# mLSTM stage: state transfers on another queue, one head after the other, and a new order of matmuls inside a weight block

## The chip, the cores and the metric

One core of one Trainium2 chip runs the whole program in one launch. The metric is the device time of an execution in microseconds, the median over runs. Five engines work side by side, each through its own instructions in order: TensorE (PE in the profile, its weight loads PEld), VectorE (DVE), ScalarE (ACT), GpSimd (POOL) and SyncE (SP). An engine whose next instruction waits holds up everything behind it. DMA transfers are issued from the queue of one of the engines; before the change, all of them from SP's.

## The reference

One inference step of a two-layer decoder trunk, for a prompt of 256 tokens and 8 samples of one token each, which share the weights. Model width 2048, everything in float32. Cut to what matters:

```python
for i in range(2):
    mix = conformer_conv(x, ...) if i == 0 else mlstm_mixer(x, ...)
    x = layer_norm(ALPHA * x + mix, ...)
    x = layer_norm(ALPHA * x + conv_ffn(x, ...), ...)
    x = x + sigmoid(x @ pl_w_gate[i]) * rms_norm(p[i] @ pl_w_proj[i], pl_g[i])

# mlstm_mixer: 8 heads, q and k of width 128, v of width 256
z = x @ w_in                       # q, k, v, output gate o, input and forget gates
...
# for each chunk of 128 tokens and each head:
s   = (q @ k.T) * exp(d - m_tok)
num = s @ v + (q @ c) * w_inter
den = max(abs(sum(s) + (q @ n) * w_inter), exp(-m_tok))
h   = num / den
c   = g_state * c + (g_tok * k).T @ v     # matrix memory, 128 x 256 a head
n   = g_state * n + sum(g_tok * k)
...
hn  = (h - mean(h)) * rsqrt(var(h) + eps) * hn_g
out = (sigmoid(o) * hn) @ w_out + b_out
```

Each of the 8 samples brings its own matrix memory `c` for each head (8 x 8 x 128 x 256 floats, 8 MB), which is read, multiplied with q, updated and written back.

## The kernel before

Activations lie feature by feature: 128 features on the partitions, 264 columns (256 prompt tokens and 8 samples). A float32 product is made of three faster ones: the input is split in a high and a low part (XH, XL), each weight chunk too (`whi` on ACT, L238; `wlo` on DVE, L239), and TensorE adds high by high (L254), high by low input (L256 and L263) and low weight by high (L257) into one accumulator.

`wblock` (L203) does one block: 512 output features, four accumulators `acc` of 128 features, the input features in chunks of 128 (`kc`), two chunks to a half (four where the block is 256 wide). Weights come by `raw` tiles over SP's queue. `side` is a table from a chunk's number to functions that are called ahead of that half: in this way norms of the heads are put between the matmuls of a block. Six PSUM banks serve the accumulators, so a block's third and fourth accumulator take the banks that the first and second of the block before it leave. `lag` and `stage` are variants for the first blocks behind a layer norm and the last ahead of one.

The order on each engine is not the program's: a planner with a simulated timeline places the instructions by priority and by when it expects their inputs. `tc.high_priority` moves weight splits and evictions ahead. `after(a, b)` fixes that `a` stands behind `b` in order, without a wait.

The mLSTM stage (`mlstm`, L668) works on four pairs of heads. `project(pr)` makes q and k (one block), then v (one block), with evictions to `qk` (L905, L907) and `vv` (L925) on ACT. `heads(pr)` runs two `Head` objects through `turns`, which takes one step of each generator in turn: `prompt` (exponentials L770, scores, transposes, numerators, denominators, the prompt's final state) and `sample` (the products with the samples' states). `opened(pr)` makes the output gate (L943), `Head.norm` the norm over a head in three steps (`hm` L874, `hq` L882, then square root, reciprocal and product), and `gated` multiplies and splits into XH, XL as the input of `ml_w_out`. `out_blocks` (L444) does four blocks of 512 features and adds each into X (the residual).

During the heads the memory of X is lent out: X itself is put in DRAM (`xscr`, L695) and comes back ahead of `out_blocks` (L980). The lent room holds the samples' states `Ct` and the rows of q and k, `kb`, broadcast to all partitions: for each head two halves (`b4`) of four samples with a buffer each. The two heads of a pair, and all pairs, use the same two buffers in turn:

```python
for b4 in range(2):
    Ct, kb = ...                       # X's room
    dma.dma_start(Ct, I["cT"][h, :, 4 * b4:4 * b4 + 4])
    dma.dma_start(kb, rows[h, 4 * b4:4 * b4 + 4].partition_broadcast(P))
    ...                                # qp = Ct * q, sum -> qc       (DVE, L847, L849)
    ...                                # kb = k * v, eight copies     (ACT, L853)
    ...                                # Ct = Ct * f + kb, four       (DVE, L856)
    dma.dma_start(O["cT"][h, :, 4 * b4:4 * b4 + 4], Ct)
    yield
```

Of the kernel before, what the change touches and what calls it, by code (L numbers as in the profile page):

```python
# [14 lines left out]
AF = mybir.ActivationFunctionType  # L15
# [92 lines left out]
def _body(ctx, tc, nc, I, O):  # L108
# [85 lines left out]
                big.tile([P, 8, T], dt, name=name + "1", tag="hB1"))  # L194

    def split(hi, lo, src):
        s.copy(hi, src)
        tt(lo, src, f32(hi), ALU.subtract)

    wdma, wlast = [None], [None]  # L200

# [1 line left out]
    def wblock(W, cols, rhs, nk, acc, k0=0, loe=None, hook=None, fine=False, native=None, hold=(), lag=0, stage=0, side=None):  # L203
        behind, late = [], []
        width = sum(w for _, w in cols)
        nm = width // P
        kq = 4 if width == 256 else 2
        for kg in range(0, nk, 2 * kq):
            kn = min(2 * kq, nk - kg)
            raw = rawp.tile([P, 4, 512], F32, name="raw")  # L210
            if width == 256:
                raw = raw.rearrange("p a (b m) -> p (a b) m", b=2)
            for ka, step in ([(k, 2) for k in range(0, kn, 2)] if fine else [(0, kn)]):
                if hook:
                    hook(kg + ka, step)
                at = 0
                for c0, w in cols:
                    wdma[0] = dma.dma_start(raw[:, ka:ka + step, at:at + w],
                                  W[(k0 + kg + ka) * P:(k0 + kg + ka + step) * P, c0:c0 + w]
                                  .rearrange("(k p) m -> p k m", p=P))  # L220
                    at += w
            for h0 in range(0, kn, kq):
                for f in (side or {}).get(kg + h0, ()):
                    f()
                if native and native(kg + h0):
                    for kc in range(kg + h0, kg + h0 + kq):
                        for j in range(nm):
                            pe.matmul(acc[j], raw[:, kc - kg, j * P:(j + 1) * P], X[:, kc], start=kc == 0,  # L228
                                      stop=kc == nk - 1)
                    continue  # L230
                hi = hlp.tile([P, 2, 512], F32R, name="whi")
                lo = hlp.tile([P, 2, 512], F32R, name="wlo")
                if width == 256:
                    hi, lo = (w.rearrange("p a (b m) -> p (a b) m", b=2) for w in (hi, lo))
                r = raw[:, h0:h0 + kq, :width]
                e = loe(kg + h0) if loe else v
                with tc.high_priority(AHEAD):
                    whi = s.copy(hi[:, :, :width], r)  # L238
                    wlo = e.tensor_tensor(lo[:, :, :width], r, f32(hi[:, :, :width]), ALU.subtract)  # L239
                for k, first in hold:  # L240
                    if kg + h0 >= k:
                        after(whi, first[0])
                        after(wlo, first[1])
                if nk - kg - h0 <= stage:

                    late.append((kg + h0, hi, lo))
                    continue
                for k2 in range(kq):
                    kc = kg + h0 + k2
                    xh, xl = rhs(kc)  # L250
                    for j in range(nm):
                        wh = hi[:, k2, j * P:(j + 1) * P]
                        wl = lo[:, k2, j * P:(j + 1) * P]
                        pe.matmul(acc[j], wh, xh, start=kc == 0, stop=False)  # L254
                        if kc and not lag:
                            pe.matmul(acc[j], wh, xl, start=False, stop=False)  # L256
                        wlast[0] = pe.matmul(acc[j], wl, xh, start=False, stop=not lag and kc == nk - 1)  # L257
                    if kc == 0 or lag:
                        behind.append((kc, [hi[:, k2, j * P:(j + 1) * P] for j in range(nm)], xl))
                    while behind and (kc >= behind[0][0] + lag or kc == nk - 1):  # L260
                        k0_, whs, xl = behind.pop(0)
                        for j in range(nm):
                            pe.matmul(acc[j], whs[j], xl, start=False, stop=lag > 0 and k0_ == nk - 1)  # L263
        for j in range(nm if late else 0):
            for ka, hi, lo in late:
                for k2 in range(2):
                    xh, xl = rhs(ka + k2)
                    wh, wl = (w[:, k2, j * P:(j + 1) * P] for w in (hi, lo))
                    pe.matmul(acc[j], wh, xh, start=False, stop=False)
                    pe.matmul(acc[j], wh, xl, start=False, stop=False)  # L270
                    pe.matmul(acc[j], wl, xh, start=False, stop=ka + k2 == nk - 1)
# [396 lines left out]
    def mlstm(xin):  # L668
# [79 lines left out]
        NP = smp.tile([P, NH], F32, name="NP")  # L748
        NS = smp.tile([P, NH, NB], F32, name="NS")

        class Head:


            def __init__(self, h, j, qk, vv, H):
                self.h, self.q, self.k, self.v, self.H = h, qk[:, j], qk[:, 2 + j], vv[:, 2 * j:2 * j + 2], H
                self.bc = bc = s0[:, j * RP:(j + 1) * RP]
                dma.dma_start(bc, scr[h:h + 1, :].partition_broadcast(P))
                self.bw, self.ben, self.bwi, self.bwf = (bc[:, 256:384], bc[:, 384:648], bc[:, 648:656],
                                                         bc[:, 656:664])
                e = s0[:, 2 * RP + j * T:2 * RP + (j + 1) * T]  # L760
                self.E, self.den = e[:, :SEQ].rearrange("p (n l) -> p n l", n=2), e
                self.P = s1[:, j * 256:j * 256 + 256].rearrange("p (n l) -> p n l", n=2)
                self.vtag = ("sf", "fo")[j]

            def prompt(self):
                h, q, k, vh, E, Pt, H, den = self.h, self.q, self.k, self.v, self.E, self.P, self.H, self.den
                tt(E, self.bc[:, 0:SEQ].rearrange("p (n l) -> p n l", n=2),
                   mask.unsqueeze(1).to_broadcast([P, 2, L]), ALU.add)
                for n in range(2):
                    act(E[:, n], E[:, n], AF.Exp, bias=AT[:, n, h:h + 1], scale=-1.0)  # L770
                yield
                ps = misc("S")
                for n in range(2):
# [43 lines left out]
            def sample(self):  # L817
# [20 lines left out]
                yield  # L838
                qc = smp.tile([P, NB, 2], F32, name="qc", bufs=2)
                for b4 in range(2):  # L840
                    Ct, kb = (XF[:, o + b4 * 1024:o + b4 * 1024 + 1024].rearrange("p (b x k) -> p b x k", b=4, x=2)
                              for o in (0, 2048))
                    dma.dma_start(Ct, I["cT"][h, :, 4 * b4:4 * b4 + 4])
                    dma.dma_start(kb, rows[h, 4 * b4:4 * b4 + 4].partition_broadcast(P))
                    for b2 in (0, 2):
                        qp = s1[:, 512 + 4 * T:1024 + 4 * T].rearrange("p (b x k) -> p b x k", b=2, x=2)
                        ins = tt(qp, Ct[:, b2:b2 + 2], kb[:, b2:b2 + 2, 0:1, :].to_broadcast([P, 2, 2, P]), ALU.mult)  # L847
                        after(ins, self.pt)
                        v.tensor_reduce(qc[:, 4 * b4 + b2:4 * b4 + b2 + 2], qp, AX.X, ALU.add)  # L849
                    for bi in range(4):  # L850
                        e = 4 * b4 + bi
                        for x in range(2):
                            act(kb[:, bi, x], kb[:, bi, 1], AF.Copy, scale=vw[:, x, e:e + 1])  # L853
                    for bi in range(4):
                        e = 4 * b4 + bi
                        stt(Ct[:, bi], Ct[:, bi], bwf[:, e:e + 1], kb[:, bi], ALU.mult, ALU.add)  # L856
                    dma.dma_start(O["cT"][h, :, 4 * b4:4 * b4 + 4], Ct)
                    yield
                hs = H[:, :, SEQ:]
                tt(hs, qc.rearrange("p b x -> p x b"), bwf.unsqueeze(1).to_broadcast([P, 2, NB]), ALU.mult)  # L860
                sv = smp.tile([P, 2, NB], F32, name="sv", bufs=2)
# [37 lines left out]
        def project(pr, first=None, second=None):  # L899
# [22 lines left out]
            acc = proj([(2048 + pr * 512, 512)], second)  # L922
            with tc.high_priority(AHEAD):
                for j in range(4):
                    s.copy(vv[:, j], acc[j])  # L925
            return qk, vv

        def heads(pr, qk, vv):
# [3 lines left out]
                Hs = s1[:, 512:512 + 4 * T].rearrange("p (x t) -> p x t", x=4)  # L932
            hd = [Head(2 * pr + j, j, qk, vv, Hs[:, 2 * j:2 * j + 2]) for j in range(2)]
            turns([x.prompt() for x in hd] + [x.sample() for x in hd])
            return Hs, [x.norm() for x in hd]

        def opened(pr, side=None):

# [7 lines left out]
        def gated(pr, Hs, so, js):  # L946
            for j in js:
                c = 4 * pr + j
                stt(Hs[:, j], Hs[:, j], pc("ml_hn_g", c), so[:, j], ALU.mult, ALU.mult)
                split(XH[:, c], XL[:, c], Hs[:, j])  # L950

        def normed(*gens):

# [4 lines left out]
            return side  # L958

        p0 = project(0)  # L960
        h0, n0 = heads(0, *p0)
        so = opened(0)
        p1 = project(1, normed((n0[0], 6)), normed((n0[1], 6)))
        gated(0, h0, so, range(4))
        h1, n1 = heads(1, *p1)
        so = opened(1)
        p2 = project(2, normed((n1[0], 6)), normed((n1[1], 6)))
        gated(1, h1, so, range(4))
        h2, n2 = heads(2, *p2)
        p3 = project(3, None, normed((n2[0], 0), (n2[1], 6)))  # L970
        h3, n3 = heads(3, *p3)
        so = opened(2)
        gated(2, h2, so, range(4))
        so = opened(3, normed((n3[0], 6)))
# [2 lines left out]
        side[10] = side[10] + [lambda: gated(3, h3, so, range(2, 4))]  # L977
        dma.dma_start(O["np"], NP)
        dma.dma_start(O["ns"], NS)
        dma.dma_start(X, xscr)  # L980
        return out_blocks(I["ml_w_out"][0], rhs_of((XH, XL)), NC, 0, True, 3, side=side)


# [169 lines left out]
```

## Time and profile before

| | us |
|---|---|
| median of 3 runs | 2551.62 |
| lowest, highest run | 2549.35, 2553.93 |
| the profiled execution's own time | 2550.97 |
| its span, first to last instruction | 2549.2 |
| TensorE busy | 2511.8 |
| VectorE busy | 1606.6 |
| ScalarE busy | 1262.0 |
| GpSimd busy | 281.0 |

The mean granted TensorE clock is 0.997. The mLSTM stage lies at about 1255 to 1600 us of the span. A busy TensorE only says that it had matmuls in work; the time that can be won stands in its waits and in the granted clock, so these are the views to read. In a row of waits, "PE hq L882 <- DVE hq L137" reads: TensorE, at the matmul of line 882 that writes `hq`, waited for VectorE's instruction of line 137 that writes its input. L137, L140 and L197 are helpers, so there the tile's name tells which step it is.

### The profile page before, as it was taken

The page shows a single profiled execution, that of the slowest core. Times are in us where ns is not written, and L with a number is a line of the kernel's source. Part 1 is how long each engine was busy: PE and PEld are TensorE (multiplying, and loading weights), DVE is VectorE, ACT ScalarE, POOL GpSimd, SP SyncE. Part 2 cuts the span into 40 slices and gives each one's busy share as a digit, 9 for nine tenths or more (in the row PEclk, how much of TensorE's full clock was granted, in tenths as well). Part 3 has the DMA queues.
Part 4 walks back from the last instruction along what each step waited for, and adds up shares of the span by engine and source line. Part 5 has one row for each costly group of instructions (what it writes and reads, how often), then busy time and mean ns, then how long its engine had stood idle before and what let it go on. Part 6 is the DMA issues. An engine that isn't in the chain of part 4 may idle for free.

```text
span 2549.2 us, 47224 instructions
## 1 busy us (share of the span) xinstructions
PE 2511.8 (99%) x19980; PEld 2482.3 (97%) x19980; DVE 1606.6 (63%) x2381; ACT 1262.0 (50%) x1783; POOL 281.0 (11%) x227
## 2 busy tenths in 40 slices
PE   8999999999999999999999999999999999999999
PEld 8998999999999999999989998999999999999999
DVE  4899685555445555488667787675555445555595
ACT  6547474444334444366457665464444334444363
POOL 6986020000000000020000000020000000000020
PEclk9999999999999999999999999999999999999999
DMA  6556546555555556546677777555555555556554
GB/s 225 186 164 215 196 146 199 182 179 173 185 178 180 181 182 210 182 159 194 212 240 244 248 245 254 190 171 182 182 173 184 178 179 181 182 182 205 182 170 135
DMA packets 270535, 486.54 MB, mean 191 GB/s; under 512 B 12107, under 2 KB 72267, under 8 KB 269779
## 3 DMA queue, kind: packets, MB, share of 16 engines
q1 hardware_dynamic: 270322, 483.52, 58.2%
q8 instruction: 156, 2.56, 0.4%
q14 instruction: 57, 0.46, 0.1%
HBM read 465.77 MB, written 19.68 MB: 190 GB/s over the span
## 4 chain that ended last, share of the span: by engine, by line
PE 89%; DVE 4%; DMA 4%; ACT 2%; POOL 1%; issue 1%; SPq 0%; DVEq 0%; POOLq 0%; ACTq 0%
PE acc L254 28%; PE acc L257 28%; PE acc L256 25%; PE acc L263 3%; DVE Y L140 1%; PE acc L228 1%; PE acc L493 1%; DMA raw<-in_cv_w_in 1%; DMA spare<-scr 1%; DMA out_cT<-X 1%; DMA X<-in_cT 1%; PE acc L640 1%; DVE wlo L239 1%; ACT whi L238 0%; POOL cscr L137 0%
## 5 line engine op out<-in xcount | busy, mean ns | idle before, releaser
L239 DVE TENSOR_TENSOR wlo<-raw,whi 128x1024 fp32r<-128x1024 f32 x742 | 913.4, 1236 | 789.9 <-ACT whi L238 741.6
L238 ACT CAST whi<-raw 128x1024 fp32r<-128x1024 f32 x792 | 827.0, 1048 | 1014.5 <-PE acc L256 955.1
L254 PE MATMUL acc<-XH,whi 128*128 128x264 f32 x4128 | 1150.6, 286 | 2.9 <-ACT whi L238 1.5
L257 PE MATMUL acc<-XH,wlo 128*128 128x264 f32 x4128 | 1142.2, 285 | 5.0 <-POOL wlo L239 3.4
L256 PE MATMUL acc<-XL,whi 128*128 128x264 f32 x3560 | 1007.7, 284 | 0.0
L257 PEld LDWEIGHTS acc<-XH,wlo 128*128 128x128 f32 x4128 | 772.5, 189 | 6.2 <-POOL wlo L239 3.8
L254 PEld LDWEIGHTS acc<-XH,whi 128*128 128x128 f32 x4128 | 773.0, 189 | 5.5 <-ACT whi L238 2.1
L256 PEld LDWEIGHTS acc<-XL,whi 128*128 128x128 f32 x3560 | 673.5, 189 | 0.4
L239 POOL TENSOR_TENSOR wlo<-raw,whi 128x1024 fp32r<-128x1024 f32 x50 | 121.7, 2444 | 1718.7 <-DVE X L137 1506.0
L257 PE MATMUL acc<-ha,wlo 128*128 128x264 f32 x1024 | 290.0, 285 | 0.0
L254 PE MATMUL acc<-ha,whi 128*128 128x264 f32 x1024 | 288.4, 285 | 0.0
L256 PE MATMUL acc<-ha,whi 128*128 128x264 f32 x960 | 271.9, 284 | 0.0
L254 PE MATMUL acc<-xo,whi 128*128 128x264 f32 x768 | 221.4, 289 | 2.9 <-ACT vv L925 1.7
L257 PE MATMUL acc<-xo,wlo 128*128 128x264 f32 x768 | 218.9, 287 | 0.0
L256 PE MATMUL acc<-xo,whi 128*128 128x264 f32 x720 | 207.6, 288 | 0.0
L257 PEld LDWEIGHTS acc<-ha,wlo 128*128 128x128 f32 x1024 | 193.1, 189 | 0.0
L254 PEld LDWEIGHTS acc<-ha,whi 128*128 128x128 f32 x1024 | 191.9, 188 | 0.1
L256 PEld LDWEIGHTS acc<-ha,whi 128*128 128x128 f32 x960 | 181.3, 189 | 0.1
L254 PEld LDWEIGHTS acc<-xo,whi 128*128 128x128 f32 x768 | 144.6, 188 | 4.0 <-ACT vv L925 1.9
L257 PEld LDWEIGHTS acc<-xo,wlo 128*128 128x128 f32 x768 | 144.7, 189 | 0.6
L140 DVE SCALAR_TENSOR_TENSOR Y<-U,par,Y 128x242 f32<-128x242 f32 (+12 forms) x335 | 131.2, 454 | 11.5 <-ACT u L597 6.8
L256 PEld LDWEIGHTS acc<-xo,whi 128*128 128x128 f32 x720 | 135.9, 189 | 0.6
(289 smaller groups left out, 2516.1 us busy)
## 6 DMA issues: line engine op xcount, KB each, us to landing
raw<-in_ff_w_gate SPq DMA_DIRECT2D x88, 1024.0 KB, 5.1
raw<-in_ff_w_up SPq DMA_DIRECT2D x88, 1024.0 KB, 5.1
raw<-in_ff_w_down SPq DMA_DIRECT2D x88, 1024.0 KB, 5.0
raw<-in_pl_w_gate SPq DMA_DIRECT2D x32, 1024.0 KB, 5.0
raw<-in_ml_w_in SPq DMA_DIRECT2D x32, 1024.0 KB, 6.9
raw<-in_cv_w_in SPq DMA_DIRECT2D x60, 512.0 KB, 5.1
raw<-in_cv_w_out SPq DMA_DIRECT2D x16, 1024.0 KB, 5.0
raw<-in_ml_w_in SPq DMA_DIRECT2D x32, 512.0 KB, 4.6
```

Source lines behind the costliest of these rows:

```text
L140: return v.scalar_tensor_tensor(o, a, sc, b, op0, op1)
L228: pe.matmul(acc[j], raw[:, kc - kg, j * P:(j + 1) * P], X[:, kc], start=kc == 0, stop=kc == nk - 1)
L238: whi = s.copy(hi[:, :, :width], r)
L239: wlo = e.tensor_tensor(lo[:, :, :width], r, f32(hi[:, :, :width]), ALU.subtract)
L254: pe.matmul(acc[j], wh, xh, start=kc == 0, stop=False)
L256: pe.matmul(acc[j], wh, xl, start=False, stop=False)
L257: wlast[0] = pe.matmul(acc[j], wl, xh, start=False, stop=not lag and kc == nk - 1)
L263: pe.matmul(acc[j], whs[j], xl, start=False, stop=lag > 0 and k0_ == nk - 1)
L493: po(pe.matmul(acc, w[:, k, j * P:(j + 1) * P], pt[:, k], start=k == 0, stop=k == 1))
L640: pe.matmul(acc[:, 30 - t:SEQ], diag[c0 + j, t], U4[j][:, 0:226 + t], start=t == t0, stop=t == t0 - pt + 1)
```

## The change

- **Matmul order.** In a block without a lag, the halves are now used output by output: for each accumulator all chunks of the half (high by high, high by low, low by high), then the next accumulator. Before: chunk by chunk, and for each chunk accumulator by accumulator; the high-by-low products of chunk 0 came behind its others.
- **Exponentials.** The exponentials of `prompt` are ordered behind `out[0]`, the last eviction of `vv` of the pair.
- **State transfers.** Loads of `Ct`, broadcasts of `kb` and stores of `Ct` are issued from Pool's queue (`g`). The `yield` at the end of each half is gone, so both halves of a head come ahead of those of the pair's other head. The buffers lie elsewhere in X: each is one quarter of X, that is 4 chunks: `kb` in the first two, `Ct` in the last two.
- **Head 7.** Its two state updates (copies, multiply-adds, store) are collected in `rest` and emitted in `finish`, behind the last `gated`, and ordered behind its last split (`fence`).
- **X back.** In four quarters on Pool's queue, emitted in `finish`, where it was one transfer on SP's queue ahead of `out_blocks`.

```diff
     def split(hi, lo, src):
-        s.copy(hi, src)
-        tt(lo, src, f32(hi), ALU.subtract)
+        return s.copy(hi, src), tt(lo, src, f32(hi), ALU.subtract)
...
+                if not lag:
+                    for j in range(nm):
+                        for k2 in range(kq):
+                            kc = kg + h0 + k2
+                            xh, xl = rhs(kc)
+                            wh, wl = (w[:, k2, j * P:(j + 1) * P] for w in (hi, lo))
+                            pe.matmul(acc[j], wh, xh, start=kc == 0, stop=False)
+                            pe.matmul(acc[j], wh, xl, start=False, stop=False)
+                            wlast[0] = pe.matmul(acc[j], wl, xh, start=False, stop=kc == nk - 1)
+                    continue
                 for k2 in range(kq):
                     kc = kg + h0 + k2
                     xh, xl = rhs(kc)
                     for j in range(nm):
-                        wh = hi[:, k2, j * P:(j + 1) * P]
-                        wl = lo[:, k2, j * P:(j + 1) * P]
-                        pe.matmul(acc[j], wh, xh, start=kc == 0, stop=False)
-                        if kc and not lag:
-                            pe.matmul(acc[j], wh, xl, start=False, stop=False)
-                        wlast[0] = pe.matmul(acc[j], wl, xh, start=False, stop=not lag and kc == nk - 1)
-                    if kc == 0 or lag:
-                        behind.append((kc, [hi[:, k2, j * P:(j + 1) * P] for j in range(nm)], xl))
+                        pe.matmul(acc[j], hi[:, k2, j * P:(j + 1) * P], xh, start=kc == 0, stop=False)
+                        wlast[0] = pe.matmul(acc[j], lo[:, k2, j * P:(j + 1) * P], xh, start=False, stop=False)
+                    behind.append((kc, [hi[:, k2, j * P:(j + 1) * P] for j in range(nm)], xl))
...
                 for n in range(2):
-                    act(E[:, n], E[:, n], AF.Exp, bias=AT[:, n, h:h + 1], scale=-1.0)
+                    after(act(E[:, n], E[:, n], AF.Exp, bias=AT[:, n, h:h + 1], scale=-1.0), out[0])
...
                 for b4 in range(2):
                     Ct, kb = (XF[...]...
-                              for o in (0, 2048))
-                    dma.dma_start(Ct, I["cT"][h, :, 4 * b4:4 * b4 + 4])
-                    dma.dma_start(kb, rows[h, 4 * b4:4 * b4 + 4].partition_broadcast(P))
+                              for o in ((8 + 4 * b4) * T, 4 * b4 * T))
+                    g.dma_start(Ct, I["cT"][h, :, 4 * b4:4 * b4 + 4])
+                    g.dma_start(kb, rows[h, 4 * b4:4 * b4 + 4].partition_broadcast(P))
...
-                    dma.dma_start(O["cT"][h, :, 4 * b4:4 * b4 + 4], Ct)
-                    yield
+                    def update(b4=b4, Ct=Ct, kb=kb, back=(None, None)):
+                        ...            # the copies behind back[0], the multiply-adds behind back[1]
+                        g.dma_start(O["cT"][h, :, 4 * b4:4 * b4 + 4], Ct)
+
+                    if h == NH - 1:
+                        self.rest.append(update)
+                    else:
+                        update()
...
-                    s.copy(vv[:, j], acc[j])
+                    out[0] = s.copy(vv[:, j], acc[j])
...
-                split(XH[:, c], XL[:, c], Hs[:, j])
+                fence[:] = split(XH[:, c], XL[:, c], Hs[:, j])
...
-        dma.dma_start(X, xscr)
+        def finish():
+            for f in rest:
+                f(back=fence)
+            for q in range(0, NC, 4):
+                g.dma_start(X[:, q:q + 4], xscr[:, q:q + 4])
+
+        side[10].append(finish)
```

More of the change, by code (lines that the diff above doesn't have):

```diff
@@ L262, in wblock @@
                         for j in range(nm):
-                            pe.matmul(acc[j], whs[j], xl, start=False, stop=lag > 0 and k0_ == nk - 1)
+                            pe.matmul(acc[j], whs[j], xl, start=False, stop=k0_ == nk - 1)
         for j in range(nm if late else 0):
@@ L749, in mlstm @@
         NS = smp.tile([P, NH, NB], F32, name="NS")
+        out, fence = [None], [None, None]
         class Head:
@@ L763, in __init__ @@
                 self.vtag = ("sf", "fo")[j]
+                self.rest = []
             def prompt(self):
@@ L840, in sample @@
                 for b4 in range(2):
-                    Ct, kb = (XF[:, o + b4 * 1024:o + b4 * 1024 + 1024].rearrange("p (b x k) -> p b x k", b=4, x=2)
-                              for o in (0, 2048))
-                    dma.dma_start(Ct, I["cT"][h, :, 4 * b4:4 * b4 + 4])
-                    dma.dma_start(kb, rows[h, 4 * b4:4 * b4 + 4].partition_broadcast(P))
+                    Ct, kb = (XF[:, o:o + 1024].rearrange("p (b x k) -> p b x k", b=4, x=2)
+                              for o in ((8 + 4 * b4) * T, 4 * b4 * T))
+                    g.dma_start(Ct, I["cT"][h, :, 4 * b4:4 * b4 + 4])
+                    g.dma_start(kb, rows[h, 4 * b4:4 * b4 + 4].partition_broadcast(P))
                     for b2 in (0, 2):
@@ L849, in sample @@
                         v.tensor_reduce(qc[:, 4 * b4 + b2:4 * b4 + b2 + 2], qp, AX.X, ALU.add)
[L850 to L856, printed above, removed]
-                    dma.dma_start(O["cT"][h, :, 4 * b4:4 * b4 + 4], Ct)
-                    yield
+                    def update(b4=b4, Ct=Ct, kb=kb, back=(None, None)):
+                        for bi in range(4):
+                            e = 4 * b4 + bi
+                            for x in range(2):
+                                ins = act(kb[:, bi, x], kb[:, bi, 1], AF.Copy, scale=vw[:, x, e:e + 1])
+                                if back[0]:
+                                    after(ins, back[0])
+                        for bi in range(4):
+                            e = 4 * b4 + bi
+                            ins = stt(Ct[:, bi], Ct[:, bi], bwf[:, e:e + 1], kb[:, bi], ALU.mult, ALU.add)
+                            if back[1]:
+                                after(ins, back[1])
+                        g.dma_start(O["cT"][h, :, 4 * b4:4 * b4 + 4], Ct)
[3 more added lines that the diff above has]
+                        update()
                 hs = H[:, :, SEQ:]
@@ L934, in heads @@
             turns([x.prompt() for x in hd] + [x.sample() for x in hd])
-            return Hs, [x.norm() for x in hd]
+            return Hs, [x.norm() for x in hd], hd[1].rest
         def opened(pr, side=None):
@@ L960, in mlstm @@
         p0 = project(0)
-        h0, n0 = heads(0, *p0)
+        h0, n0, _ = heads(0, *p0)
         so = opened(0)
@@ L964, in mlstm @@
         gated(0, h0, so, range(4))
-        h1, n1 = heads(1, *p1)
+        h1, n1, _ = heads(1, *p1)
         so = opened(1)
@@ L968, in mlstm @@
         gated(1, h1, so, range(4))
-        h2, n2 = heads(2, *p2)
+        h2, n2, _ = heads(2, *p2)
         p3 = project(3, None, normed((n2[0], 0), (n2[1], 6)))
-        h3, n3 = heads(3, *p3)
+        h3, n3, rest = heads(3, *p3)
         so = opened(2)
```

## The prediction

> **What bounds the kernel now.** First the page, for the engines' shares; then the waits of TensorE, cut to the mLSTM stage; then its windows, and the chain of waits through it.
>
> ```profile
> span 2549.2 us, 47224 instructions
> PE 2511.8 (99%) x19980; PEld 2482.3 (97%) x19980; DVE 1606.6 (63%) x2381; ACT 1262.0 (50%) x1783; POOL 281.0 (11%) x227
> ```
>
> TensorE is the bound: no edit lowers its number of matmuls, so the change can win only the 37.4 us (2549.2 - 2511.8) in which it sits idle, and the time in which it runs slowly. The waits of TensorE from 1255 to 1600 us (us in total, times, longest):
>
> ```profile
> PE hq L882 <- DVE hq L137: 5.0, 2, 2.9
> PE acc L254 <- ACT vv L925: 1.7, 1, 1.7
> PE num L803 <- ACT spare L809: 1.6, 1, 1.6
> PE acc L257 <- DVE wlo L239: 1.6, 2, 1.3
> PE hm L874 <- DVE hm L137: 1.1, 1, 1.1
> PE acc L254 <- ACT qk L905: 0.9, 1, 0.9
> PE acc L254 <- ACT XH L197: 0.8, 1, 0.8
> PE rows L915 <- DVE NS L137: 0.4, 1, 0.4
> PE acc L254 <- ACT so L943: 0.3, 1, 0.3
> ```
>
> They come to 13.4 us, over a third of all idle time, and everything the change touches but the matmul order lies in this stage. Where (window, us, busy time and count of PE, PEld, DVE, ACT, POOL; granted clock, DMA share, GB/s):
>
> ```profile
> 1277.00:1312.00 35.00, 31.66 (x255) 31.02 (x255) 27.80 (x62) 23.83 (x63) 0.00 (x0) 1.00 0.66 221
> 1557.00:1593.00 36.00, 30.67 (x226) 29.28 (x225) 27.17 (x43) 16.16 (x28) 0.00 (x0) 0.95 0.78 279
> 1617.00:1640.00 23.00, 23.00 (x191) 23.00 (x191) 13.21 (x15) 8.03 (x9) 0.00 (x0) 1.00 0.55 183
> ```
>
> The third is an undisturbed block: 0.120 us a matmul, 192 of them 23.1 us. The second, the first output block with head 7's norm inside it, loses 5.3 us idle and runs at clock 0.95, which is 36 x 0.05 = 1.8 us more. The chain of waits (start, us, what) says what is late there:
>
> ```profile
> 1278.47 0.39 ACT spare L770
> 1278.86 0.82 ACT vv L925 x3
> ...
> 1287.99 6.12 DMA out_cT<-X
> 1294.13 4.26 DMA X<-in_cT
> ...
> 1399.13 3.51 DMA out_cT<-X
> ...
> 1558.52 9.36 DMA out_cT<-X
> 1567.90 5.10 DMA X<-in_cT
> ...
> 1582.30 1.72 DVE hq L887
> ...
> 1585.98 0.92 PE acc L254 x4
> ...
> 1590.75 0.49 PE acc L254 x4
> ```
>
> The pattern is the same each time: one sample state is stored, only then is the next one loaded into the same buffer, and the head's norm, which TensorE needs, waits behind it. In the last pair the last load lands at 1573, so the norms of heads 6 and 7 run at 1577 to 1591, when chunks 12 to 15 are already due as inputs. Right after that stall four matmuls take 0.92 us, later 0.49: half speed. [...]
>
> **The change part by part.**
>
> *Pairs output by output.* In blocks without a lag the two weight chunks of a half are now used output by output, where the outputs changed fastest. The matmuls are the same in number and size: 0. What moves is when an accumulator is done. With 4 outputs of 6 matmuls in the last half, the first is complete 18 matmuls before the block's end instead of 9, and the third output of the next block, which takes its bank, starts 12 matmuls in instead of 4 (chunk 0 was done hi and lo first). The time allowed for an eviction goes from 13 x 0.120 = 1.6 to 30 x 0.120 = 3.6 us. So the waits on the evictions (vv 1.7, qk 0.9, so 0.3) shrink to nothing: 2.9 us. What it could cost: the second input chunk of a half is wanted 9 matmuls, 1.1 us, earlier; only the gated chunks 14 and 15 are ever near their use, and below they come 4 us ahead.
>
> *Exponentials behind evictions.* Eight pairs of exponentials now stand behind the last vv eviction of their own pair. ACT waited in order at the first pair: the exponential (1278.47) stood before the evictions (1278.86). That is the same 1.7 us, not counted twice. What stands behind the exponentials now: the score product on DVE, and kg and vt on ACT. Each pair issues 4 of 0.4 us and perhaps a table load:
>
> ```profile
> L770 ACT ACT_TABLE_LOAD x6 | 7.7, 1283 | 0.1
> L770 ACT ACTIVATE spare<-spare,AT 128x128 f32<-128x128 f32 x16 | 5.6, 395 | 7.1 <-DVE spare L137 7.0
> ```
>
> That is 4 x 0.4 + 1.3 = 2.9 us after the evictions. The cover is other blocks' matmuls between scores and numerators, 13 us in the chain:
>
> ```profile
> 1367.10 0.89 PE S L775 x8
> ...
> 1380.90 0.44 PE num L803 x4
> ```
>
> So 0.
>
> *Head by head, on Pool's queue.* For each head and half: one load of C, one broadcast of k and q, one store. That is 48 transfers off SP's queue and onto Pool's, and the reload of X, one transfer of 2112 KB, becomes four of 528. SP's waits in the stage, and the transfers (KB, median us to landing):
>
> ```profile
> SPq L843 <- DMA out_cT<-X: 34.5, 11, 5.7
> ...
> X<-in_cT SPq DMA_DIRECT2D x16, 512.0 KB, 5.2
> X<-rows SPq DMA_DIRECT2D x16, 512.0 KB, 5.5
> out_cT<-X SPq DMA_DIRECT2D x16, 512.0 KB, 5.2
> ```
>
> SP stood 34.5 us in the first of its waits alone, each time for a store to land before the next load, with weight loads queued behind, but weights cost TensorE only part of 1.6 us (wlo above), so relieving SP is worth little by itself. [...]
>
> The gain is in the order. Before, the halves went head A first half, head B first half, A second, B second, with a `yield` between: B's first half waits for A's store, and A's second half stands behind it on DVE and ACT. Two store-and-load rounds of some 10.4 us (6.12 + 4.26) lie in a row for each pair. After, A's halves run together, then both of B's: one round. That is about 10 us earlier per pair, where the waits to be covered are at most 2.9 us (hq). POOL has no work in these windows (0.00 busy), so what is queued behind a waiting store on Pool is only the next state's load, which must wait anyway. So hq 5.0, hm 1.1, wlo 1.6, XH 0.8 go, 8.5 us, and with the stall the slow clock, 1.8.
>
> Pool's price for issuing a transfer is in no row. The nearest are SP's own landings, 3.51 to 9.36 us; I take 5.2, and keep 9.4 for the far end. ACT's waits bound what a late load does to the work behind it:
>
> ```profile
> ACT X L853 <- DVE spare L137: 23.5, 16, 6.0
> ```
>
> Sixteen waits, 6.0 the longest, and one of them reached TensorE: num, 1.6. With both of B's halves now waiting for one round in each pair, I leave that 1.6 standing and add a second one. Bounds: -1.6 (none left) to 4 x 6.0.
>
> *Last state update behind the last norm.* Head 7's 16 ACT copies and 8 DVE updates leave the stretch before its norm, where DVE was 27.17 of 36 us busy, and come behind the split of chunks 14 and 15 (the fence). That helps hq as counted. It makes something else late: X is the states' buffer, and its first quarter can be reloaded only after the first of the two updates.
>
> ```profile
> L853 ACT ACTIVATE X<-X,vw 128x128 f32<-128x128 f32 x128 | 42.4, 398 | 23.6 <-DVE spare L137 23.5
> L140 DVE SCALAR_TENSOR_TENSOR X<-X,spare 128x256 f32<-128x256 f32 x64 | 29.1, 490 | 0.0
> ```
>
> Counting from the output block's start: the hq matmul stands behind 72 matmuls, 8.7 us; a table load is 1.3; from the reciprocal (1582.30 in the chain) to the matmul with its gated chunk (1585.98) it was 3.7; for the hq matmuls, the square root, the second chunk and the splits between I add an estimated 2.3. That puts the fence at 16. Chunks 14 and 15 are due at 168 matmuls, 20.2: no wait. Then 8 copies, which start every 0.3 us, and a weight cast (1.0), and the last updates (1.0): 20.6. Issue 0.5 and landing 5.2: 26.3. Needed: DVE adds the block's result into X[0:4], and TensorE wants the bank back at 23.1 + 12 x 0.120 = 24.5, less 0.4 for the add. Late by 2.2 us. Bounds: a landing of 3.5 us leaves 0.5; one of 9.4, with the second update's 3.6 ahead of it on Pool, gives 10.0, and the clock's 1.8 with it. [...]
>
> **Sum.** Gone: 2.9 + 8.5 + 1.8 = 13.2. New: 2.2 for X and 1.6 for one more num. Net 9.4 us. The profiled execution took 2550.97 us (span 2549.2 and 1.8 around it): 2541.6. It stands 0.65 under the median of the runs, 2551.62, so 2542.2.
>
> **The rivals.**
>
> *X comes back late.* The wait in front of the second output block is 10.0 + 1.8 instead of 2.2: 2542.2 + 9.6 = 2551.8, no change. For: the store of 9.36 us happened at this very place, with DMA share 0.78. Against: the quarters are small, and the first depends on one update only. 0.15, spread from 2547 up.
>
> *The norms stay late.* If the round of store and load, not the order, set the chain, only the evictions' 2.9 is won: 2551.6 - 2.9 = 2548.7. For: one round remains in each pair. Against: about 10 us saved where 2.9 was missing. 0.12.
>
> *Pool's transfers hold up ACT and DVE in order (slower).* The place: the product of state and q for head B in each of the four pairs, with the L853 copies and then the numerators' evictions queued behind it. At 6.0 us a pair, four pairs cost 24: 2551.6 - 13.2 + 24 = 2562.4. It decides for slower from (13.2 + 5.1) / 4 = 4.6 us a pair. For: this is how 1.6 came about, and nothing shows Pool's speed. [...] 0.11.
>
> **How the numbers follow.** The forecast has 0.62. This kernel's runs (2549.35 to 2553.93) tell 0.2%, 5.1 us, from no change, so faster means under 2546.5. The forecast alone runs from 2537, with neither new wait, to 2547. Faster: 0.60 of the forecast, 0.05 of the late X, 0.04 of the late norms: 0.69. Slower: 0.11, with 0.01 from the late X: 0.12. Same: 0.19. The range 2536 to 2552 leaves out the slower rival and little else; its lower end is all 13.2 and num's 1.6 won, 2551.6 - 14.8 = 2536.8.
>
> **What would show it.** Right: no wait of TensorE on vv, qk or so; hq and hm waits under 1 us; clock 1.00 in the first output block; state transfers on Pool's queue with landings near 5 us; L853 waits of ACT well below 23.5. The X term shows as a wait of the second output block on DVE's add, itself on a Pool transfer, of 0.5 to 10 us. Wrong: a num wait in several pairs, or an hq wait as before. Outside 1255 to 1600 us nothing should move by over 1 us.

## The result, and the profile after

| | before | after |
|---|---|---|
| median, us | 2551.71 (6 runs) | 2531.77 (6 runs) |
| ratio, 95% interval | | 0.9919 (0.9909 to 0.993) |
| span of the profiled execution, us | 2549.2 | 2527.3 |

The change is faster by 0.8%, some 20 us. The forecast was 2542.2, with the lower end at 2536: right in sign, half in size.

The page of the changed kernel, its first lines:

```profile
span 2527.3 us, 47217 instructions
PE 2503.0 (99%) x19980; PEld 2476.9 (98%) x19980; DVE 1606.3 (64%) x2381; ACT 1265.0 (50%) x1779; POOL 309.5 (12%) x279
```

The same 19980 matmuls. All waits of TensorE that the trace of the changed kernel shows, over the whole span:

```profile
PE acc L227 <- DMA raw<-in_cv_w_in: 4.6, 2, 4.0
PE lnq L397 <- DVE lnq L137: 3.8, 3, 1.3
PE lnm L397 <- ACT cscr L594: 3.0, 1, 3.0
PE acc L256 <- POOL wlo L238: 2.8, 2, 1.7
PE acc L254 <- ACT whi L237: 1.9, 1, 1.9
PE lnm L397 <- DVE lne L137: 1.7, 1, 1.7
PE acc L262 <- ACT XH L414: 0.5, 2, 0.3
```

None lies in the mLSTM stage. The nine that stood there before, 13.4 us, are gone, num and rows among them. The windows of the changed kernel say the same: at the first pair's heads, over head 7's norm with the first output block, and over the 6 us behind that block.

```profile
1268.00:1303.00 35.00, 35.00 (x288) 34.77 (x287) 29.65 (x66) 25.42 (x63) 3.71 (x7) 1.00 0.89 322
1535.00:1571.00 36.00, 36.00 (x294) 35.80 (x293) 27.41 (x36) 24.71 (x42) 2.35 (x5) 1.00 0.65 218
...
1569.00:1575.00 6.00, 6.00 (x52) 6.00 (x51) 2.64 (x4) 0.56 (x1) 1.59 (x3) 1.00 0.87 257
```

TensorE is busy throughout, and the clock is 1.00 where it was 0.95.

To see where the time went, the chain of waits has four marks that recur in every version: the group of 20 matmuls in each layer norm. Before, then after:

```profile
343.25 4.45 PE acc L493 x20
1124.15 4.45 PE acc L493 x20
1664.41 4.45 PE acc L493 x20
2445.22 4.45 PE acc L493 x20
```

```profile
341.57 4.45 PE acc L498 x20
1120.88 4.45 PE acc L498 x20
1643.62 4.45 PE acc L498 x20
2423.08 4.45 PE acc L498 x20
```

From the second mark to the third lies the mLSTM stage: 540.26 us before, 522.74 after, 17.5 less. The two convolutional FFNs, first to second and third to fourth, take 780.90 and 780.81 before, 779.31 and 779.46 after: 1.6 and 1.35 less, though the change has no edit there but the matmul order. Ahead of the first mark it is 1.7; the windows there, before and then after, differ in the granted clock:

```profile
215.00:230.00 15.00, 12.08 (x50) 10.34 (x49) 14.89 (x31) 10.15 (x19) 14.37 (x14) 0.89 0.75 227
215.00:230.00 15.00, 12.01 (x59) 10.62 (x58) 14.89 (x31) 10.36 (x20) 14.45 (x13) 1.00 0.78 244
```

The states' transfers on Pool's queue (KB, median us to landing):

```profile
X<-in_cT POOLq DMA_DIRECT2D x16, 512.0 KB, 6.0
X<-rows POOLq DMA_DIRECT2D x16, 512.0 KB, 7.2
out_cT<-X POOLq DMA_DIRECT2D x16, 512.0 KB, 5.2
X<-xscr POOLq DMA_DIRECT2D x4, 528.0 KB, 7.3
```

They are no faster than SP's 5.2 to 5.5; the broadcasts are slower (7.2 beside 5.5). What is shorter is the wait behind them: ACT's copies stood 23.5 us for their inputs before, now 4.3.

```profile
ACT X L863 <- DVE spare L137: 4.3, 7, 1.2
```

### The profile page after: what moved, and what is told of

It is laid out like the page before. It is cut to its first block, busy times and chain, and to the rows that moved or that the text cites. A ratio compares the mean times of both kernels' runs of the same rounds, so it can differ in the third digit from the quotient of the medians.

```text
span 2527.3 us, 47217 instructions
## 1 busy us (share of the span) xinstructions
PE 2503.0 (99%) x19980; PEld 2476.9 (98%) x19980; DVE 1606.3 (64%) x2381; ACT 1265.0 (50%) x1779; POOL 309.5 (12%) x279
## 4 chain that ended last, share of the span: by engine, by line
PE 94%; DVE 3%; ACT 1%; DMA 1%; POOL 1%; issue 0%; SPq 0%; POOLq 0%; DVEq 0%; ACTq 0%
PE acc L255 28%; PE acc L254 28%; PE acc L256 28%; PE acc L268 2%; PE acc L262 2%; PE acc L263 2%; DVE Y L140 2%; PE acc L227 1%; PE acc L498 1%; PE acc L645 0%; DMA X<-in_xT 0%; POOL cscr L137 0%; DVE lnq L137 0%; PE num L811 0%; ACT whi L237 0%
## 5 line engine op out<-in xcount | busy, mean ns | idle before, releaser
L255 PE MATMUL acc<-XL,whi 128*128 128x264 f32 x3808 | 1077.5, 284 | 0.0
L254 PE MATMUL acc<-XH,whi 128*128 128x264 f32 x3808 | 1074.1, 285 | 1.9 <-ACT whi L237 1.9
L256 PE MATMUL acc<-XH,wlo 128*128 128x264 f32 x3808 | 1066.9, 285 | 2.8 <-POOL wlo L238 2.8
L254 PEld LDWEIGHTS acc<-XH,whi 128*128 128x128 f32 x3808 | 715.9, 189 | 3.0 <-ACT whi L237 2.3
L255 PEld LDWEIGHTS acc<-XL,whi 128*128 128x128 f32 x3808 | 717.8, 188 | 0.5
L256 PEld LDWEIGHTS acc<-XH,wlo 128*128 128x128 f32 x3808 | 710.5, 188 | 3.5 <-POOL wlo L238 3.3
L255 PE MATMUL acc<-ha,whi 128*128 128x264 f32 x1024 | 290.4, 284 | 0.0
L254 PE MATMUL acc<-ha,whi 128*128 128x264 f32 x1024 | 288.7, 284 | 0.0
L254 PE MATMUL acc<-xo,whi 128*128 128x264 f32 x768 | 223.5, 291 | 0.0
L255 PE MATMUL acc<-xo,whi 128*128 128x264 f32 x768 | 220.5, 287 | 0.0
L255 PEld LDWEIGHTS acc<-ha,whi 128*128 128x128 f32 x1024 | 192.7, 188 | 0.1
L254 PEld LDWEIGHTS acc<-ha,whi 128*128 128x128 f32 x1024 | 192.0, 189 | 0.1
L254 PEld LDWEIGHTS acc<-xo,whi 128*128 128x128 f32 x768 | 144.8, 189 | 0.7
L255 PEld LDWEIGHTS acc<-xo,whi 128*128 128x128 f32 x768 | 144.7, 188 | 0.8
```

The costliest lines, as they stand in the source:

```text
L256: wlast[0] = pe.matmul(acc[j], wl, xh, start=False, stop=kc == nk - 1)
```

## The experiments

Every ratio is against runs of the kernel before on the same chip, whose medians were 2550.4 to 2551.8; the bracket is its 95% interval. First come parts put alone on the kernel before, then parts undone in the changed one. Of the parts, the exponentials, the last update and the four quarters of X were not tried alone.

**The matmul order alone.** The new `if not lag` branch of `wblock`, nothing else.

> The kernel before with the new matmul order alone. Theory (the matmul order gives the evictions room in the mLSTM stage, 2.9 us, and is the only edit that can explain the 5 us won outside that stage, at the layer norms and the first blocks): 2551.7 - 8 = 2543.7 us; TensorE's waits on vv, qk and so are gone, those on hq and hm (6 us) stay. Rival (the 5 us outside come from the planner's other placement of the whole program, not from the order itself, and the evictions' waits were cured by the exponentials): 2549 to 2552 us, and the waits on vv and qk stay.

2541.36 us, ratio 0.9968 (0.9956 to 0.998). Its waits in the stage:

```profile
PE hq L888 <- DVE hq L137: 4.4, 2, 2.9
...
PE acc L257 <- DVE wlo L239: 1.5, 2, 1.3
PE hm L880 <- DVE hm L137: 1.4, 2, 0.8
PE acc L255 <- ACT vv L931: 1.1, 2, 0.9
```

Qk and so are gone, vv shrank but did not go; the norms are as late as before (head 7's hq still waits 2.9 us). Its marks are 340.18, 1119.48, 1656.13 and 2435.59, so the FFNs take 779.30 and 779.46 us: to 0.01 us those of the whole change. The 3 us there are the matmul order's and no chance of the planner. Of the rest, 3.6 us lie between the second and third mark and 3.1 ahead of the first, where this execution, too, lacks the slow clock of the kernel before: the 60 matmuls from 219.54 us on take 12.20 us, as the same 60 do in the changed kernel, where the kernel before took 13.89.

**Head by head alone.**

```diff
                     dma.dma_start(O["cT"][h, :, 4 * b4:4 * b4 + 4], Ct)
-                    yield
```

> The kernel before with one edit alone: no step between the two halves of a head. Theory (this is the edit that brings the norms in time; the kernel with the old matmul order and all the rest was 16 us faster, and the rest is worth nothing): waits on hq and hm gone, 2535 to 2538 us; the wait on vv at the first pair, 1.7 us, stays, since nothing moves the exponentials. Rival (without the new matmul order or the last update moved, the two heads' states still come late): 2540 to 2545 us.

2542.91 us, ratio 0.9968 (0.9956 to 0.998): in the range of the rival, but for another reason. The states do come in time: the wait on hm and head 7's on hq are gone, and the 1.3 us left on hq lie at the third pair. But the evictions are worse. Waits of TensorE in the stage, then ACT where the output gate of the first pair should be evicted:

```profile
PE acc L254 <- ACT so L942: 3.2, 1, 3.2
PE acc L254 <- ACT vv L924: 2.1, 2, 1.8
PE hq L881 <- DVE hq L137: 1.3, 1, 1.3
```

```profile
1308.01 1.28 ACT L853 ACTIVATE X<-X,vw 128x128 f32<-128x128 f32 x4 [3.09 <-DVE spare L137]
1310.08 0.42 ACT L869 ACTIVATE spare<-spare 128x264 f32<-128x264 f32 x1 [0.79 <-DVE spare L137]
```

ACT waits 3.09 us in order for head B's copies, and the evictions of `so` (1314.27) queue behind. In the kernel before, TensorE's wait on `so` was 0.3 us in all.

**Both edits, and nothing else.**

> The kernel before with two edits alone: the new matmul order, and no step between the halves of a head (SP's queue, the old places of the buffers, X in one transfer, exponentials free, last update in place). Theory (these two edits make nearly the whole gain): 2529 to 2533 us. Rival (the head-by-head order gains only with the last update out of the way, or with the exponentials ordered): 2536 to 2541 us, with waits on hq, or on vv.

2530.57 us, ratio 0.9913 (0.9899 to 0.9928). The whole gain, with SP's queue, X in one transfer, exponentials free and the last update in place. Against the kernel before on the same chip the two alone are worth 9.0 and 8.2 us, 17.2; together it is 21.3. The 4 us between are about what the three intervals leave open, but the traces speak for them: in head by head alone, late evictions cost 5.3 us (so 3.2, vv 2.1), and with the room of the new matmul order 0.9. Of the stage's waits remain:

```profile
PE acc L255 <- ACT vv L930: 0.9, 2, 0.5
PE S L781 <- DVE ss L137: 0.2, 1, 0.2
```

**Both, and the exponentials ordered.**

> The two edits together (new matmul order, no step between the halves of a head) and the exponentials behind the last vv eviction; SP's queue, X in one transfer, last update in place. Theory (the two edits make the gain, and the exponentials take the 0.9 us of waits on vv that the two alone still show): 2528.5 to 2530.5 us, no wait on vv, as fast as the whole change or 1 to 3 us faster. Rival (Pool's queue and the moved last update are worth something after all): 2533 us or more.

2530.76 us, ratio 0.9919 (0.9906 to 0.9933). The waits on vv are gone, a wait of 2.2 us on the score products' input came in their place (PE S on DVE ss), and nothing was won. Beside it on the same chip the whole change again:

> The changed kernel once more, on the same chip as the reduced version, as its yardstick: 2531 to 2533 us by every theory.

2530.51 us, ratio 0.9919 (0.9905 to 0.9932). So the parts that these reduced versions leave out come, together, to nothing that can be measured.

**Pool's queue alone.** Loads, broadcasts and stores with `g.dma_start`, on the kernel before.

> The kernel before with one edit alone: loads, broadcasts and stores of the sample states on Pool's queue (order of halves, buffers, reload of X and matmul order as before). Theory (the queue is worth nothing, the states' order sets the norms): 2549 to 2553 us, waits on hq and hm as before, 6 us. Rival 1 (SP's 34.5 us of waits for stores were what made the states late): waits on hq under 2 us, 2543 to 2547 us. Rival 2, slower (a state transfer from Pool's queue lands in some 6 us at the median in the changed kernel's trace, against 5.2 to 5.5 from SP's, so with two rounds in a row the norms come later still): 2553 to 2558 us.

2550.79 us, ratio 1.0 (0.9991 to 1.0009). Nothing. SP's 34.5 us of waits for stores were free.

**The matmul order undone** in the changed kernel.

> The changed kernel with the old matmul order. Theory (order is worth 5 us outside the mLSTM stage and 2.9 inside): 2531.8 + 8 = 2539.8 us, with waits on qk and so back, and the layer norms behind the first and second stage as late as before. Rival (the mLSTM edits alone make everything but the 5 us outside): 2536.8 us, no wait on evictions. Second rival (planner): 2531.8 us, no change.

2535.9 us, ratio 0.9945 (0.9931 to 0.996): 14.5 us won, where the whole change wins 20; nearest to the first rival. In the stage only 0.7 us of an hq wait, no eviction is late. The marks of this version give 540.26 - 523.56 = 16.7 us won in the stage (1123.99 to 1647.55), and FFNs of 780.83 and 780.80, as before. So without the new matmul order the other edits do count: they bring some 6 us over head by head alone. Which of exponentials, queue and last update does it was not separated.

**SP's queue** in the changed kernel, all `g.dma_start` of the states and X back to `dma.dma_start`.

> The changed kernel with all state transfers and the four quarters of X on SP's queue. Theory (the order of the heads is what counts, the queue little): 2532 to 2535 us, no wait on hq or hm over 1 us. Rival (the queue counts: on SP each transfer stands behind weight loads and holds up others while it waits): the waits on hq and hm return with 5 to 8 us, 2537 to 2541 us.

2528.62 us, ratio 0.9915 (0.99 to 0.993), as fast as the change; no wait of TensorE on hq or hm. The lowest median of all, but the ratio is inside the interval of the change.

**Half by half** in the changed kernel: the `yield` put back behind each half.

> The changed kernel with the step between the two halves of a head put back, so that the order is first half of A, first half of B, second of A, second of B, all on Pool's queue. Theory (two store-and-load rounds in a row instead of one made the norms late): the waits on hq and hm return, 6 to 10 us with the clock, 2538 to 2542 us. Rival (Pool's queue alone made the states early enough): 2532 us, no wait on hq or hm.

2548.67 us, ratio 0.9993 (0.9984 to 1.0003): 17 us lost by one word, more than the theory's 6 to 10, and 7 us worse than the matmul order alone. Waits of TensorE from 1540 to 1620 us:

```profile
PE acc L254 <- DVE X L137: 5.3, 1, 5.3
PE hq L901 <- DVE hq L137: 2.9, 1, 2.9
```

The late norm is back, and behind it the last update and the reload of X, which the changed kernel puts behind that norm: the 5.3 us are the rival "X comes back late", set off by the states' order. Behind the two waits TensorE works some 8 us at a granted clock of 0.50, which is 4 us more; the execution's mean granted clock is 0.996, the changed kernel's 0.998.

**The exponentials freed** in the changed kernel (`after(..., out[0])` taken off).

> The changed kernel without the ordering of the exponentials behind the last vv eviction. Theory (the new matmul order gives evictions 3.6 us, which covers an exponential in front of them): 2531 to 2533 us, no wait on vv over 0.5 us. Rival (an exponential that waits for its broadcast rows blocks ACT for 3.3 us and more, and the first pair's vv is late again): 1 to 2 us more, 2533 to 2534 us, with a wait on vv.

2531.69 us, ratio 0.9915 (0.9899 to 0.9932). As the theory had it; the profiled execution shows a 0.4 us wait on vv, and one of 1.5 on hq at the third pair.

**The last update in place** in the changed kernel (`if h == NH - 1` taken off, `update()` always).

> The changed kernel with head 7's state update where those of the other heads are, X still in four quarters. Theory (with both heads' halves together, the last states are early enough, so moving the last update gave nothing): 2530 to 2533 us, no wait on hq. Rival (16 ACT copies and 8 DVE updates in front of the norm delay it): a wait on hq of 1 to 3 us with up to 1.8 for the clock, 2533 to 2537 us.

2530.8 us, ratio 0.9915 (0.9901 to 0.993): the theory's time. The profiled execution shows a wait on hq, but not the one that the rival named:

```profile
1487.07 0.64 PE L897 MATMUL hq<-hq,onesD 128*128 128x264 f32 x1 [2.83 <-DVE hq L137]
```

That is a norm of the third pair, some 70 us ahead of head 7's (1558.6), which waits for nothing. This execution took 2534.73 us, the other three 2529.4 to 2531.4, so the wait need not stand in those. Why the third pair's norm is late here, and by 0.7 to 1.5 us in several other versions, is open.

**X in one transfer** in the changed kernel.

```diff
-            for q in range(0, NC, 4):
-                g.dma_start(X[:, q:q + 4], xscr[:, q:q + 4])
+            g.dma_start(X, xscr)
```

> The changed kernel with X back in one transfer of 2112 KB instead of four quarters. It has to wait for the second store, which landed at 1576.6 us in the changed kernel's profile, and takes some 9 us, so X[0:4] comes at about 1586 instead of 1574.4. Theory (TensorE hides a late X only as far as the planner can pull the first two accumulators of the next block ahead: five halves, 7.3 us, by the five weight buffers; before, X was 5 us behind the block's end and hidden): a wait of 8 to 10 us with up to 1.8 for the clock, 2540 to 2543 us. Rival (X is not needed so early, other work is put ahead): 2532 us.

2541.58 us, ratio 0.9955 (0.994 to 0.997), 10 us lost, in the theory's range. Waits of TensorE and of DVE, and the window from 1582.3 us on:

```profile
PE acc L254 <- DVE X L137: 6.5, 1, 6.5
...
DVE X L137 <- DMA X<-xscr: 10.7, 1, 10.7
...
1582.32:1589.15 6.83, 4.21 (x19) 4.21 (x20) 1.45 (x4) 0.00 (x0) 0.00 (x0) 0.50 0.09 40
```

The wait is 6.5 us, shorter than the theory's 8 to 10; 4.2 us of work at half clock cost 2.1 more, and 1.2 us of a wait on hq stand at the third pair.

With the last update moved, X in one transfer comes too late. With the update in place it need not: the two edits alone have X in one transfer and no such wait. The quarters pay for a cost that the moved update makes.

## Why the prediction was right or wrong

**What failed**, in short, are three terms: two new waits, 3.8 us, that did not come; the time that TensorE loses in the stage, read 2.3 us too low; and 0 for the matmul order outside the stage, where it won 3 us. Without the two waits, and with the num wait gone, the sum reaches 2536.8 us; the rest lies mostly in the other two.

**Right:** the bound, the stage, and the mechanism of the largest term. The chain's pattern of store, load, norm was the cause: with one round instead of two, hm and head 7's hq are gone, in head by head alone too, and half by half brings the loss back. Issuing from Pool is worth nothing by itself, as the row on `wlo` had it (relieving SP worth little): the ratio is 1.0 with Pool's queue alone, and with SP's queue in the changed kernel 0.9915, where the change has 0.9919. The slower rival, Pool's transfers holding up ACT and DVE, found no ground; ACT's longest wait at the copies is 1.2 us, where 4.6 a pair was its point of decision.

**The two new waits, 3.8 us, were the first wrong step.** X did come late, later than reckoned: its first quarter, issued at 1568.2 us, took 6.3 us and not 5.2 (Pool's issue, taken as 0.5 without a row, took 0.53). DVE's waits in the changed kernel, from 1545 to 1600 us, and DVE's order there:

```profile
DVE X L137 <- DMA X<-xscr: 3.4, 1, 3.4
...
1574.51 1.45 DVE L137 TENSOR_TENSOR X<-acc,X 128x264 f32<-128x264 f32 x4 [3.36 <-DMA X<-xscr]
```

But TensorE did not wait, 52 matmuls in the 6 us of the window from 1569 us. The step took TensorE's order as written: third accumulator 12 matmuls into the next block. The planner does not keep it. The order of the built program, as accumulator and count of matmuls:

```
... acc0 6, acc1 6, acc2 6, acc3 6     last half of the first output block
acc0 6, acc1 6   (five times, over five halves)
acc2 6, acc3 6   (then the same halves for these)
```

Sixty matmuls, 7.2 us, go to the two accumulators whose banks are free. In the version with X whole it does not suffice, and TensorE waits 6.5 us. Counted by this order in the changed kernel's trace, the first output block's last matmul starts at 1568.31, the third accumulator of the next block at 1575.67, and DVE's first add ends at 1574.94. So X may come some 7 us behind the block before it costs anything, not 1.4, and only 0.7 us of that was left. The planner had done the same in the kernel before: 36 matmuls of its second output block stand ahead of head 7's last norm matmul. The second num wait did not come either, and the first, with rows, left (2.0 us): ACT's waits at the copies, taken for its cause, fell from 23.5 to 4.3.

**The ceiling was read too low.** Waits and clock came to 15.2 us, and the stage lost 17.5. A listed wait is shorter than what TensorE loses: a matmul counts as busy for 285 ns, but the next could start after 120, as in the undisturbed block, where 191 start in 23.00 us.

```profile
L254 PE MATMUL acc<-XH,whi 128*128 128x264 f32 x3808 | 1074.1, 285 | 1.9 <-ACT whi L237 1.9
```

So each of the 11 waits hides up to 0.165 us, 1.8 in all. Counted from start to start between the two marks, all gaps above 0.14 us lose 36.3 us before and 19.1 after, which is 17.2 of the 17.5; the rest is the size that the shorter matmuls of the next point make.

**"Outside 1255 to 1600 us nothing should move by over 1 us"** was wrong, and so was the cost of 0 for the matmul order. The first FFN's stretch is 1.6 to 1.7 us shorter and the second's 1.35 to 1.4 wherever the new order runs, and never without it. Each has 6096 matmuls in the new order (21 blocks of 192, and 2064 in the down projection): 0.22 to 0.28 ns each. From start to start, over 200 us inside the second FFN, the mean is 121.7 to 121.9 ns before and with head by head alone, 121.5 to 121.6 with the matmul order alone and after, at a granted clock of 1.00 in both. What it is inside TensorE stays open: the accumulator changes every 6 matmuls instead of every 3.

The 1.7 us ahead of the first mark go mostly with the clock. In the windows from 215 to 230 us TensorE does 50 matmuls before and 59 after; a clock of 0.89 over 15 us is worth 1.65 us. This slow stretch comes and goes among versions with the new order. The four that have it where the kernel before does (half by half, exponentials freed, last update in place, X in one transfer) have the mark at 342.56 to 343.26; the kernel before and three others with the old order have it at 343.16 to 343.75. That leaves about half a microsecond for the edits. What decides whether the stretch comes is not shown.

The sum put right: 9.4 + 3.8 + 2.0 + 2.3 in the stage is 17.5, and 1.6 + 1.35 + 1.7 outside, less 0.2 behind the last mark, make 21.9, the difference of the spans. The medians differ by 2 us less, mostly since the profiled execution after (2529.56) was the fastest of its six.

**The eviction term**, 2.9 us, was the right mechanism but counted as if alone. Its worth seems larger in company: as far as the traces show, it carries what head by head does to ACT.

## What to carry to other kernels

Ask first in which order tasks share a buffer: two halves of one task back to back leave one round of store and load between tasks, where interleaved halves make two in a row, and the other queue did not repair that here (half by half on Pool's queue: 2548.67 us). A matmul order that finishes accumulators early buys room for whatever engine evicts them (put in alone, it took TensorE's waits on evictions in the stage from 2.9 to 1.1 us), and may be worth more beside an edit that crowds that engine. Where a planner orders TensorE, price a late input by how much other ready work it can pull ahead (free banks times buffered weights), not by the program's order (here sixty matmuls, 7.2 us, and not twelve), and take waits of a pipelined engine as lower bounds (here 15.2 us of waits and clock for 17.5 lost).

## What the runs showed of the hardware

In each of the four layer norms one VectorE operation took over five times as long beside a weight split on GpSimd: 2.20 to 2.48 us, where `lne` and `lnq` otherwise take 0.42 to 0.43. At the layer norm of the first mark, DVE and then POOL, before:

```profile
338.68 0.43 DVE L137 TENSOR_TENSOR X<-acc,X 128x264 f32<-128x264 f32 x1
339.15 2.45 DVE L137 TENSOR_TENSOR lne<-X 128x264 f32<-128x264 f32 x1
...
338.96 2.35 POOL L239 TENSOR_TENSOR wlo<-raw,whi 128x1024 fp32r<-128x1024 f32 x1 [77.45 <-ACT whi L238]
```

and after:

```profile
337.87 0.43 DVE L137 TENSOR_TENSOR lne<-X 128x264 f32<-128x264 f32 x1
338.61 2.20 DVE L137 TENSOR_TENSOR lnq<-lnq 128x264 f32<-128x264 f32 x1 [0.30 <-ACT lnq L376]
...
338.02 2.50 POOL L238 TENSOR_TENSOR wlo<-raw,whi 128x1024 fp32r<-128x1024 f32 x1 [77.76 <-ACT whi L237]
```

The operation that starts during Pool's weight split takes 2.45 or 2.20 and ends 0.29 us behind it; before it was `lne`, after `lnq`. The other three layer norms show the same (2.44 to 2.48 us). What holds it up is not shown. It stands in the chain of waits of each layer norm, is still there in the changed kernel, and no run here tried to move it.
